# Sixteen stores of a transformer block issued by ScalarE instead of SyncE

## The chip, the cores and the metric

The kernel runs on one core of a Trainium2 chip. Its time is device microseconds of one launch. Before the change it takes 1237.1 us, the median of three runs (1236.84 to 1238.23). A run is told from no change here from about 0.2% on, 2.5 us.

A core has five engines with an instruction stream each, and each stream runs strictly in its own order. The profile calls them PE (TensorE, matrix products; its weight loads are listed as PEld), DVE (VectorE), ACT (ScalarE), POOL (GpSimd) and SP (SyncE, which in this kernel only issues transfers). "SPq" is SyncE's stream of transfer issues.

## The reference

One block over 1024 tokens of width 1024, all float32. It is cut here to what the change touches.

```python
h = rmsnorm(x, g_mix_pre[l])
proj = h @ w_in[l]
qa, ka, va, gate_a, beta_a, alpha_a, qb, kb, vb = jnp.split(proj, split_at, axis=-1)
out_a = gated_deltanet(qa, ka, va, gate_a, beta_a, alpha_a, ...)   # 4 heads of 128
out_b = dilated_attention(qb, kb, vb, rel_bias)                    # 8 heads of 64
mix = jnp.concatenate([out_a, out_b], axis=-1) @ w_out[l]
x = x + rmsnorm(mix, g_mix_post[l])
...
# inside gated_deltanet: a scan over 16 chunks of 64 tokens, then
_, o = lax.scan(step, s0, (u, w, attn, q_dec, k_dec, g_end))
o = o * lax.rsqrt(jnp.mean(o * o, axis=-1, keepdims=True) + RMS_EPS) * onorm_g
o = o * jax.nn.silu(heads(gate))
return o.reshape(Bn, S, GDN_WIDTH)
```

After the mix comes a gated feed-forward layer of width 2816. Two results matter below: the scan's normed output, and the SILU of the gate, with which it is multiplied.

## The kernel before, in words

Every matrix product takes its operands as a high and a low float32r part and sums three products of them, so most of the element-wise work consists of pairs "cast to the high part, subtract to get the low part". The tiles of 128 tokens are numbered t = 0 to 7.

**How the order comes about.** Each piece of work is a Python generator that yields one instruction after another. A planner (class Weaver) runs them all side by side when the program is built: it keeps a clock for each engine and a clock "D" for transfers, prices each instruction (class Op), and always emits the one that can start first by its clocks, ties going to the smaller priority number. Where a step may run on either of two engines (Either), it takes the one that would finish it first. The order in which the planner emits is the order in which each engine runs on the chip. A transfer's price on the issuing engine stands in one line, 166: 565 ns for SyncE and 1000 ns for anyone else. Before the change all 865 transfers are issued by SyncE, in one stream, so a transfer that waits for its data holds up all transfers emitted after it.

**The stages around the change**, with the times of the profiled execution:

- Projections (from the start to about 482 us): products of the normed input with w_in into PSUM tiles named pj. The last ones are the four gate heads in two halves, eight tiles gst of 128 x 512. They also serve as filler for TensorE beside the next stage.
- The scan (chain, lines 1388 to 1427, about 290 to 443 us): for each tile t the inputs ckq, cg, cbv and ckd are loaded; the recurrence alternates TensorE (p), VectorE (R, the state, o) and ScalarE (vn, parts of o). chain_out (lines 1434 to 1455) then squares and norms o, transposes it on TensorE (otp), has ScalarE copy it with the gain onorm into ot (two activations), and stores ot to d_mix in HBM. There is one ot buffer, shared with the squares osq.
- Attention (lines 1465 to 1667, about 290 to 525 us) beside it: loads qs, ks, strip, vn, vo and vf; scores pS, a VectorE reduction into Sr and mx, the exponential on ScalarE, transposes tp, casts ptn, pto and ptf, the value products pV, and sums plow and ptmp, stored to d_mix as well.
- Gates (lines 811 to 851): VectorE multiplies each projected tile into gst. When six are there, gate_silu runs six SILUs on ScalarE in one go and then stores six tiles to d_gt; when all eight are there, the other two follow. The first tile's gates are also used straight from SBUF.
- Output projection (lines 1694 to 1862, from about 485 us): w_out is loaded into borrowed buffers (y, gpost, gpre, wor), cast to woh and wol; d_mix and d_gt come back as mx and gt; the attention's part is divided by its sums (rtok, rt, rrow, rp); the products are pw.
- Then the residual and the norm, and the feed-forward layer (tiles bank) to the end.

The stores of ot wait for nobody until mix_load reads them back, one tile at a time, from 448.0 us on; those of gst are read back from 495.6 us on.

Of the kernel before, what the change touches and what calls it, by code (L numbers as in the profile page):

```python
# [21 lines left out]
P = 128  # L22
S = 1024
# [69 lines left out]
def _free(ap):  # L93
    n = 1
    for d in ap.shape[1:]:
        n *= d
    return n


def _run(ap):  # L100

    dims = [list(d) for d in ap.ap]
    n, dims = 1, dims if ap.space == DRAM else dims[1:]
    for st, k in reversed(dims):
        if k > 1 and st != n:
            break
        n *= k
    return n
# [34 lines left out]
class Op:  # L143


    def __init__(self, w, eng, name, fn, args, kw):
        self.eng, self.fn, self.args, self.kw = eng, fn, args, kw
        out = kw.get("out", args[0] if args else None)
        outs = [out] + ([kw["accum_out"]] if kw.get("accum_out") is not None else [])
        ins = [x for x in list(args) + list(kw.values())  # L150
               if isinstance(x, bass.AP) and not any(x is o for o in outs)]
        self.dma = name == "dma_start"
        self.table = next((x for x in args if x in (AF.Exp, AF.Silu)), None) if name == "activation" else None
        self.grow = name == "matmul" and not kw.get("start", True)
        self.ins, self.outs = [w.region(x) for x in ins], [w.region(x) for x in outs]
        n = max(_free(x) for x in ins + outs)
        if eng == "PE":
            if name == "transpose":
                c = 109.0
            elif args[2].dtype == F32R:  # L160
                c = max(_free(args[2]), 256) * 0.4414 + 3.0
            else:
                n = _free(args[2])
                c = n * 1.667 if out.shape[0] == P else 36 + 0.44 * n if n <= 64 else n * 1.0 if out.shape[0] == 64 else n * 0.45
        elif self.dma:
            c = 565.0 if eng == "S" else 1000.0
            b = 4 * min(_run(x) for x in ins + outs)
            self.move = 4.0 * _free(out) * out.shape[0] / b * (10.0 + b / 22.0) / 16.0
        elif eng == "A":
            c = 60 + (1.87 if any(x.ap[-1][0] > 3 for x in ins) else 0.83 if any(x.space == PSUM for x in ins) else 0.9) * n + 93 * (len(outs) - 1) + 85 * sum(1 for x in ins if _free(x) == 1)  # L170
        elif eng == "G":
            vals = list(args) + list(kw.values())
            c = 295 + 165.0 * n if ALU.pow in vals else (60 + 0.83 * n if name == "memset" else 140 + (1.7 if any(d[0] == 0 for x in ins for d in x.ap) else 2.1) * n)
        elif name in ("tensor_scalar", "tensor_copy", "memset") and not any(x.space == PSUM for x in ins):
            c = 65 + 0.52 * n + (60 if any(_free(x) == 1 for x in ins) and n > 1 else 0)
        elif any(abs(x.ap[-1][0]) > 3 for x in ins + outs):
            c = 65 + 1.85 * n
        elif name == "reciprocal":
            c = 70 + 8.0 * (n - 1)
        else:  # L180
            c = 65 + 1.04 * n + (60 if name == "scalar_tensor_tensor" else 0)
        self.cost, self.bias = c, 0.0

        self.rows = (args[1].shape[0], out.shape[0]) if eng == "PE" else None
        sb = sum(1 for x in ins if x.space != PSUM and _free(x) > 1)
        self.port = not self.dma and (eng == "G" and sb > 0 or eng == "V" and (
            sb > 1 or name in ("tensor_scalar", "tensor_copy") and all(x.space != PSUM for x in ins + outs) and _free(out) > 1))
# [350 lines left out]
def block_kernel(ctx: ExitStack, tc: tile.TileContext, a, out):  # L538
    nc = tc.nc
    w = Weaver(nc)  # L540
    T, V, A, G, SY = (Engine(w, e, k) for e, k in (
        (nc.tensor, "PE"), (nc.vector, "V"), (nc.scalar, "A"), (nc.gpsimd, "G"), (nc.sync, "S")))
# [5 lines left out]
    def tr(out, in_):  # L548
        return T.transpose(out, in_, ident[:])
# [33 lines left out]
    def rstd_from(pool, ss, scale, eps, tag, bufs=4):  # L583
        n = ss.shape[-1]
        m = pool.tile([P, n], F32, name=tag + "_m", bufs=bufs)
        yield V.tensor_scalar(m[:], ss, scale, eps, ALU.mult, ALU.add)
        r = pool.tile([P, n], F32, name=tag + "_r", bufs=bufs)
        yield G.tensor_tensor(r[:], m[:], mhalf[:, :n], ALU.pow)
        return r
# [6 lines left out]
    d_mix = dr.tile([KT, P, S], F32, name="d_mix")  # L596
# [214 lines left out]
    def gate(*hs):  # L811
        def sink(h, hf, ps):
            z = yield gstS[h // 2, hf].get([P, 512], F32, name="gst")
            yield V.tensor_tensor(z[:], ps[:], rb[:, hf * 512:hf * 512 + 512], ALU.mult)
            pj.put(ps)
            gates.append((z, d_gt[h, :, hf * 512:hf * 512 + 512]))
            if not hf:
                first[h] = z
            if len(gates) in BURST:
                w.spawn(gate_silu(gates[len(silued):]), 2, eager=len(gates) in EAGER)  # L820
                silued.extend(gates[len(silued):])
            if len(gates) == 8:
                ev_gates.fire()
        for hf in range(2):
            for h in hs:
                yield from proj_half(12 + h, hf, lambda hf, ps, h=h: sink(h, hf, ps))
            if len(hs) > 1:
                for b in range(2):
                    hS.put(*hT[b, hf])
# [10 lines left out]
    def gate_silu(part):  # L840
        yield [A.activation(z[:], z[:], AF.Silu) for z, _ in part]
        for z, dst in part:
            silu.add(z.tensor.name)
        if len(first) == GH and all(z.tensor.name in silu for z in first.values()):
            ev_silu.fire()
        for z, dst in part:
            yield SY.dma_start(dst, z[:])
            if z not in first.values():
                outS.put(z)
        if part[-1] is gates[-1] and len(gates) == 8:  # L850
            ev_gt.fire()
# [536 lines left out]
    def chain():  # L1388
        for t in range(NT):
# [4 lines left out]
            for c in range(2):  # L1394
# [30 lines left out]
                cp.put(p2)  # L1425
            ch.put(kq, gg, kd, bv)
            w.spawn(chain_out(o, t), 3)

    def chain_o1(o, p1, sw, us):
# [4 lines left out]
    def chain_out(o, t):  # L1434
        sq = yield ch.get([P, GH, P], F32, name="osq", tag="ot", bufs=1)
        yield A.activation(sq[:], o[:], AF.Square)
        ss = ch.tile([P, GH], F32, name="oss")
        yield V.tensor_reduce(ss[:], sq[:], AX.X, ALU.add)
        ch.put(sq)
        yield V.tensor_tensor(ss[:], ss[:], rqs2[:, t::8], ALU.mult)  # L1440
        r = yield from rstd_from(ch, ss[:], 1.0, EPS, "on", 2)
        yield V.tensor_tensor(r[:], r[:], rqsw[:, t::8], ALU.mult)
        yield V.tensor_tensor(o[:], o[:], r[:].unsqueeze(2).broadcast_to([P, GH, P]), ALU.mult)
        yield After(o[:])
        tp = yield banks.get([P, GH, 2, 64], F32, name="otp")
        yield [tr(tp[:, h, :, :], o[:, h, :]) for h in range(GH)]
        ch.put(o)
        ot = yield ch.get([P, GH, 2, 64], F32, name="ot", bufs=1)
        for c in range(2):
            yield A.activation(ot[:, :, c, :], tp[:, :, 1 - c, :], AF.Copy, scale=onorm[:])  # L1450
        banks.put(tp)
        yield SY.dma_start(d_mix[0:4, :, t * P:(t + 1) * P].rearrange("h p j -> p h j"),
                           ot[:].rearrange("p h c j -> p h (c j)"))
        ch.put(ot)
        ev_o[t].fire()
# [1016 lines left out]
```

## Time and profile before

| | |
|---|---|
| time, median of 3 runs | 1237.1 us (1236.84 to 1238.23) |
| time of the profiled execution | 1238.43 us |
| its span, first to last instruction | 1236.7 us |
| granted clock of TensorE, mean | 0.998 |
| transfers, moved in all | 865 issues by SyncE, 213.42 MB |
| ot stores to d_mix | 8 of 256 KB, from 306.3 to 442.8 us |
| gst stores to d_gt | 8 of 256 KB, from 469.5 to 491.5 us |

The profile gives busy time for each engine and for chosen stretches ("windows": PE, PEld, DVE, ACT and POOL busy us with the number of instructions, then TensorE's granted clock, the transfer engines' busy share and GB/s). A row of waits reads: who waited, for whose instruction, total us, times, longest. A row of a timeline reads: start, duration, engine, line, operation, output<-input, shape, count, and in brackets the idle time before it and what ended it. The chain of waits follows the work that ended last backwards from the end; its rows read start, duration, what. Nearly every row carries line 283, because the planner issues everything through that one line; so one goes by the names of the tiles. The duration of a transfer's issue is the time of the issuing engine only, not that of the movement.

### The profile page before, as it was taken

Reading aid. Unit: us, or ns where it says so; the run is one execution under the profiler, and the core shown is the slowest. Engines: PE = TensorE matmul, PEld = TensorE weight load, DVE = VectorE, ACT = ScalarE, POOL = GpSimd, SP = SyncE. Lnnn points to the kernel's source line nnn. Section 1 sums busy time; section 2 is a strip of 40 time slices with the busy share of each in tenths; the row PEclk is TensorE's granted clock in tenths of the full one; section 3 lists DMA queues with packets and bytes.
Section 4 is the critical chain, followed back from the end, with each engine's and each line's share of the span. In section 5 each row is a group of like instructions: output and inputs, shape, how many; then the busy total and the mean of one; then the engine's idle time right before and its main releaser. Section 6 shows DMA issues by size and latency. Waiting matters only on the chain.

```text
span 1236.7 us, 19617 instructions
## 1 busy us (share of the span) xinstructions
PE 1213.7 (98%) x6783; PEld 1015.4 (82%) x6783; DVE 962.2 (78%) x1857; ACT 575.5 (47%) x1174; POOL 190.6 (15%) x159
## 2 busy tenths in 40 slices
PE   7999999999999998999999999999999999999997
PEld 6887798888888887888788888888888887888886
DVE  4689969737999887876898877876678767976876
ACT  6545432236677757655553333333333334544541
POOL 0135321011221102111210010111001100000111
PEclk9999999999999999999999999999999999999999
DMA  7754372769877578694544433322333129744335
GB/s 261 240 154 158 111 220 83 176 213 306 251 234 255 160 235 255 201 297 158 188 142 154 137 120 128 107 72 85 120 128 120 50 94 327 247 134 153 101 121 204
DMA packets 169978, 213.42 MB, mean 173 GB/s; under 512 B 32232, under 2 KB 87016, under 8 KB 169880
## 3 DMA queue, kind: packets, MB, share of 16 engines
q1 hardware_dynamic: 169880, 212.18, 54.2%
q8 instruction: 54, 0.88, 0.3%
q14 instruction: 44, 0.36, 0.1%
HBM read 149.97 MB, written 65.95 MB: 175 GB/s over the span
## 4 chain that ended last, share of the span: by engine, by line
PE 87%; DVE 5%; DMA 4%; ACT 2%; issue 1%; POOL 1%; SPq 1%; DVEq 0%; POOLq 0%; ACTq 0%
PE bank L283 48%; PE pj L283 19%; PE pw L283 7%; PE tp L283 4%; PE p L283 3%; PE pS L283 2%; PE pV L283 2%; PE pm L283 2%; DMA xn<-in_x 1%; DMA gpre<-in_w_out 1%; SPq L283 1%; DMA ks<-d_k 0%; DMA views<-in_w_down 0%; DMA wr<-in_w_in 0%; DMA xT<-in_x_t 0%
## 5 line engine op out<-in xcount | busy, mean ns | idle before, releaser
L283 PE MATMUL pj<-hTh,w 128*128 128x512 f32 x768 | 265.9, 403 | 6.2 <-ACT hTh L283 5.3
L283 PEld LDWEIGHTS pj<-hTh,w 128*128 128x128 f32 x768 | 145.7, 190 | 37.7 <-ACT hTh L283 5.3
L283 ACT CAST wbh<-wraw 128x512 fp32r<-128x512 f32 x131 | 80.9, 622 | 199.2 <-PE bank L283 126.1
L283 PE MATMUL pj<-hTl,w 128*128 128x512 f32 x384 | 151.5, 395 | 0.0
L283 DVE TENSOR_TENSOR wbl<-wraw,wbh 128x512 fp32r<-128x512 f32 x131 | 94.1, 721 | 29.2 <-ACT wbh L283 29.1
L283 PE MATMUL bank<-views 128*128 128x512 f32 (+1 forms) x307 | 85.0, 385 | 0.0
L283 PEld LDWEIGHTS pj<-hTl,w 128*128 128x128 f32 x384 | 73.0, 190 | 11.8 <-DVE hTl L283 0.7
L283 PE MATMUL bank<-views,dah 128*128 128x512 f32 (+1 forms) x214 | 73.5, 379 | 0.0
L283 PE MATMUL bank<-dbh,views 128*128 128x512 f32 (+1 forms) x201 | 70.3, 380 | 0.0
L283 POOL TENSOR_TENSOR m<-m,m 128x512 f32<-128x512 f32 x18 | 28.3, 1574 | 251.9 <-DVE r L283 153.3
L283 PEld LDWEIGHTS bank<-views 128*128 128x128 f32 x307 | 57.4, 188 | 11.7 <-ACT views L283 0.4
L283 PE MATMUL pw<-woh,mh 128*128 128x512 f32 x128 | 51.5, 403 | 0.0
L283 PE MATMUL pw<-woh,ml 128*128 128x512 f32 x128 | 50.0, 391 | 0.0
L283 PE MATMUL pw<-wol,mh 128*128 128x512 f32 x128 | 49.9, 390 | 0.0
L283 PE MATMUL bank<-dbh,dah 128*128 128x512 f32 (+1 forms) x129 | 49.1, 381 | 0.0
L283 ACT CAST w<-wr 128x512 fp32r<-128x512 f32 x54 | 33.2, 619 | 33.9 <-PE pj L283 25.0
L283 DVE SCALAR_TENSOR_TENSOR yc<-raw,convw,yc 128x1024 f32<-128x1024 f32 x36 | 47.3, 1313 | 0.4
L283 PEld LDWEIGHTS bank<-views,dah 128*128 128x128 f32 x214 | 40.0, 188 | 7.6
L283 ACT ACTIVATE Sr<-Sr,mx 128x384 f32<-128x384 f32 (+2 forms) x64 | 38.2, 598 | 13.7 <-DVE mx L283 12.4
L283 DVE TENSOR_TENSOR w<-wr,w 128x512 fp32r<-128x512 f32 x39 | 26.5, 687 | 23.1 <-ACT w L283 22.9
L283 DVE TENSOR_TENSOR m<-bank,m 128x512 f32<-128x512 f32 x44 | 30.1, 685 | 18.2 <-PE bank L283 18.2
L283 PEld LDWEIGHTS bank<-dbh,views 128*128 128x128 f32 x201 | 37.6, 188 | 7.2
(405 smaller groups left out, 3278.1 us busy)
## 6 DMA issues: line engine op xcount, KB each, us to landing
wr<-in_w_in SPq DMA_DIRECT2D x56, 256.0 KB
wraw<-in_w_gate SPq DMA_DIRECT2D x52, 256.0 KB
wraw<-in_w_up SPq DMA_DIRECT2D x52, 256.0 KB
views<-d_hid SPq DMA_DIRECT2D x47, 256.0 KB
db<-in_w_down SPq DMA_DIRECT2D x40, 256.0 KB
qs<-d_q SPq DMA_DIRECT2D x64, 128.0 KB
da<-d_hid SPq DMA_DIRECT2D x30, 256.0 KB
d_hid<-x SPq DMA_DIRECT2D x22, 256.0 KB
```

The source lines that it names most:

```text
L283: op.fn(*op.args, **op.kw)
```

## The change

Two stores are issued by ScalarE (A) instead of SyncE (SY), and the planner is given a price of 450 ns for a transfer issued by ScalarE, where it would have been 1000. What is stored, where to and after which instruction stays the same. Since the planner works with the new engine and price, the order of everything that it emits after the first of these stores may come out differently on all engines.

```diff
@@ -163,7 +163,7 @@
         elif self.dma:
-            c = 565.0 if eng == "S" else 1000.0
+            c = {"S": 565.0, "A": 450.0}.get(eng, 1000.0)
             b = 4 * min(_run(x) for x in ins + outs)
@@ -844,7 +844,7 @@
         for z, dst in part:
-            yield SY.dma_start(dst, z[:])
+            yield A.dma_start(dst, z[:])
             if z not in first.values():
                 outS.put(z)
@@ -1449,7 +1449,7 @@
         banks.put(tp)
-        yield SY.dma_start(d_mix[0:4, :, t * P:(t + 1) * P].rearrange("h p j -> p h j"),
+        yield A.dma_start(d_mix[0:4, :, t * P:(t + 1) * P].rearrange("h p j -> p h j"),
                            ot[:].rearrange("p h c j -> p h (c j)"))
         ch.put(ot)
         ev_o[t].fire()
```

## The prediction

> **What bounds the kernel now.** I read the page first, then TensorE's waits, the busy table by stretches, the chain and the timelines around the sixteen stores. Busy shares come first.
>
> ```profile
> PE 1213.7 (98%) x6783; PEld 1015.4 (82%) x6783; DVE 962.2 (78%) x1857; ACT 575.5 (47%) x1174; POOL 190.6 (15%) x159
> PE 87%; DVE 5%; DMA 4%; ACT 2%; issue 1%; POOL 1%; SPq 1%; DVEq 0%; POOLq 0%; ACTq 0%
> ```
>
> TensorE is busy 1213.7 of 1236.7 us and carries 87% of the chain. Whatever moves between ScalarE and SyncE can gain at most TensorE's 23.0 us of idle time, so I look for where that idle time is.
>
> ```profile
> core 0: us, PE busy (x) PEld busy (x) DVE busy (x) ACT busy (x) POOL busy (x), PEclk, DMA share, GB/s
> 300.00:445.00 145.00, 144.40 (x1164) 125.10 (x1163) 133.22 (x415) 101.52 (x293) 27.37 (x25) 1.00 0.74 228
> 480.00:500.00 20.00, 16.16 (x104) 13.36 (x106) 18.42 (x45) 16.24 (x39) 5.36 (x4) 0.91 0.79 254
> 650.00:1230.00 580.00, 578.86 (x2583) 479.78 (x2581) 441.21 (x681) 217.76 (x390) 59.95 (x44) 1.00 0.42 137
> PE rt L283 <- POOL rtok L283: 3.8, 1, 3.8
> ```
>
> The scan with the attention beside it (300 to 445 us) leaves TensorE 0.60 us idle, and 650 to 1230 leaves 1.14. The only hole near the change is between 480 and 500: 3.84 us, in one wait, with a granted clock of 0.91 in that stretch. What fills the time before that hole is in the chain.
>
> ```profile
> 468.98 7.51 DMA gpre<-in_w_out
> ...
> 477.09 1.64 ACT kf L283 x2
> ...
> 486.39 0.33 PE rt L283
> ```
>
> A weight load into gpre, issued at 468.98, lands 7.51 us later; ScalarE casts it (woh) and then works off, kf copies and all, what TensorE's rt waits for. So one short stretch, about 455 to 486 us, is not bound by TensorE but by a load and by ScalarE's order. The gate stores lie in it.
>
> **The change part by part.** Sixteen issues move: eight of the scan's output (d_mix) and eight gates (d_gt).
>
> ```profile
> L283 SPq DMA_DIRECT2D d_mix<-ot x8: 365/374/378, 306.3 to 442.8; - x8
> L283 SPq DMA_DIRECT2D d_gt<-gst x8: 326/448/912, 469.5 to 491.5; - x8
> ```
>
> *Issue time.* By the medians this is 8 x 0.374 + 8 x 0.448 = 6.6 us that SyncE loses and ScalarE gains. No row shows a transfer issued by ScalarE, so SyncE's rows are the nearest; by the fastest and slowest of each row the sum lies between 5.5 and 10.3 us. Eight of them, 3.0 us, fall in 300 to 445, where ScalarE is idle for 145.00 - 101.52 = 43.5 us: 0 on the path. If that cover were gone the 3.0 us would be paid in full. Six gate stores, 6 x 0.448 = 2.7 us, come right after the six SILUs of the first burst:
>
> ```profile
> 468.23 3.24 ACT L283 ACTIVATE gst<-gst 128x512 f32<-128x512 f32 x6
> 476.56 0.62 ACT L283 CAST woh<-gpre 128x512 fp32r<-128x512 f32 x1 [5.09 <-DMA gpre<-in_w_out]
> 490.31 1.15 ACT L283 ACTIVATE gst<-gst 128x512 f32<-128x512 f32 x2
> ```
>
> ```profile
> 490.98 5.53 PE pw L283 x24
> ```
>
> ScalarE sits idle for 5.09 us there, waiting for gpre, so the 2.7 us are hidden in that wait: 0, and 2.7 if the planner gives that cast to VectorE. The last two stores, 0.9 us, hold up the casts behind 490.31, while TensorE, in the chain's row, has 24 projection matmuls up to 496.51 in hand: 0.
>
> *ScalarE's own result.* A store on ScalarE waits for the activation just before it to be written. The nearest row is SyncE's: the two ot of 430.29 end at 431.13 and the store starts at 431.16, so 0.03 us; from the other side, a queued instruction behind it may be held some 0.3 us as well. Sixteen times that is 0.5 to 5 us of ScalarE time under the same cover: 0.
>
> ```profile
> 430.29 0.84 ACT L283 ACTIVATE ot<-otp,onorm 128x256 f32<-128x256 f32 x2 [0.20 <-PE otp L283]
> 431.16 0.38 SPq L283 DMA_DIRECT2D d_mix<-ot  x1
> ```
>
> *The turn of eight.* The transfers keep a distance of eight: SyncE's store of the first scan tile stood until the eighth transfer before it had landed.
>
> ```profile
> 297.28 0.92 SPq L283 DMA_DIRECT2D cbv<-d_bv  x1
> 298.31 3.80 SPq L283 DMA_DIRECT2D qs<-d_q  x4
> 302.26 1.17 SPq L283 DMA_DIRECT2D ks<-d_k  x2
> 304.33 0.33 SPq L283 DMA_DIRECT2D strip<-d_bias  x1
> 306.26 0.38 SPq L283 DMA_DIRECT2D d_mix<-ot  x1
> SPq L283 <- DMA cbv<-d_bv: 1.5, 1, 1.5
> ```
>
> From cbv to strip there are 1 + 4 + 2 + 1 = 8, and the wait before 306.26 is for cbv. I take it that a transfer issued by ScalarE takes its turn among the same eight; then ScalarE is held, and everything queued on it behind the store: the casts ptn and pto, the exponentials Sr, the scan's vn.
>
> ```profile
> 300.61 0.84 ACT L283 ACTIVATE ot<-otp,onorm 128x256 f32<-128x256 f32 x2 [0.51 <-PE otp L283]
> 309.63 0.58 ACT L283 COPY vn<-p 64x512 f32<-64x512 f32 x1
> 310.68 1.05 PE L283 MATMUL p<-vn,ckd 128*128 128x128 f32 x8
> 301.40:309.63 8.23, 8.23 (x81) 6.76 (x79) 8.04 (x25) 5.16 (x17) 1.05 (x1) 1.00 0.97 287
> ```
>
> The worst case for this tile: ot ends at 301.45, the hold lasts until 306.2 and the issue 0.4, so 5.2 us. ScalarE has 8.23 - 5.16 = 3.1 us idle before vn, which leaves vn 2.1 us late; TensorE needs it 0.47 us after its end (310.21 to 310.68), so it loses up to 1.6 us. The best case is 0: the store is issued behind a few more instructions, or earlier in the transfers' turn. For the other fifteen the transfer eight back had landed before the result was there, so SyncE's wait, where it had one, was for ScalarE. I take 0.5 of 0 to 1.6 us, near the lower end because TensorE has filler from the projections in this stage.
>
> *What SyncE gains.* Its waits for these results end, and the loads queued behind the stores start earlier.
>
> ```profile
> SPq L283 <- ACT ot L283: 7.3, 3, 5.5
> SPq L283 <- ACT gst L283: 1.9, 3, 0.9
> ```
>
> 9.2 us of standing go from SyncE, 5.5 of them in one piece ahead of the load at 431.63. But TensorE's idle time in that stage is 0.60 us, so the gain is between 0 and 0.6: 0.
>
> *The load of gpre.* Now gpre is ahead of the six gate stores in one queue:
>
> ```profile
> q1 hardware_dynamic: 169880, 212.18, 54.2%
> 468.39 0.54 SPq L283 DMA_DIRECT2D strip<-d_bias  x1
> 468.98 0.42 SPq L283 DMA_DIRECT2D gpre<-in_w_out  x1
> 469.49 4.36 SPq L283 DMA_DIRECT2D d_gt<-gst  x6
> strip<-d_bias SPq DMA_DIRECT2D x10, 416.0 KB
> gpre<-in_w_out SPq DMA_DIRECT2D x1, 512.0 KB
> d_gt<-gst SPq DMA_DIRECT2D x8, 256.0 KB
> 471.50:476.50 5.00, 5.00 (x42) 3.94 (x42) 3.68 (x16) 0.00 (x0) 3.17 (x3) 1.00 0.94 297
> ```
>
> From 471.5 to 476.5 the engines moved 5.0 x 297 = 1.49 MB at a share of 0.94, so there is no room left. What is ahead, strip with 0.43 MB and gpre with 0.52, is at most 0.95, so at least 0.5 MB of the stores had already run beside it on engines that were done with gpre. Six stores are 6 x 256 KB = 1.57 MB. After the change they stand in a queue of ScalarE's own. If they stay behind gpre, as now, gpre lands as now: 0. If all the rest of them goes ahead of it, it lands (1.57 - 0.54) / 0.297 = 3.5 us later, and TensorE's hole grows by as much. Against this, ScalarE can do the two kf copies (1.64 us, now behind the wait) ahead of the cast. So -1.6 to +3.5; I take +0.5, as stores issued from 471.5 on come 2.5 us after gpre was queued. The Trainium skill, page "DMA: Bandwidth & Descriptors", section "Queues, rings and completion order", says that each DMA engine goes round-robin, packet by packet, between the queues that have work for it, and that SyncE and ScalarE have a queue each. By that rule gpre shares from 471.5 on, the term would be near its upper end, and the sum would come out near 1241; no row of before can show it, as there is one queue.
>
> *The order.* The planner's price for a transfer of ScalarE's, 450 ns, costs nothing by itself, but from the first store on a new order is worked out for all engines. Later stretches have only 1.14 us to win; I count 0, with 2 us either way.
>
> The sum: 0.5 + 0.5 = +1.0 us. The profiled execution took 1238.43 us, 1.73 beyond its span and 1.33 above the median of 1237.1; its sum would be 1239.4. Against the median this gives 1238.1 us. About 0.2%, or 2.5 us, is what a measurement can tell from no change, so this is no difference.
>
> **The rivals.** *The stores delay gpre (slower).* Place: the hole before rt. Price: up to 3.5 us on gpre, one for one on TensorE, since ScalarE's work behind woh has no other slack up to 486.39; with the 0.5 of the first tile +3 to +4, so 1240.1 to 1241.1 us. It decides from the point where gpre lands over 2.5 us later than 7.51 after its issue. For it: the share of 0.94, and the rule of taking turns above. Against: gpre's head start. Chance 0.24.
>
> *ScalarE is held by the turn of eight in several tiles (slower).* For it: each hold stops an engine on which the recurrence waits, and a transfer can take as long as gpre to land, 7.51 us. Against: only one of the sixteen waited on it at SyncE. Two or three tiles at 1.6 us make 1240.3 to 1241.9. Chance 0.09.
>
> *The hole closes (faster).* With the cast of gpre off the head of ScalarE's queue, or the stores fully inside the idle 5.09 us and the later casts on VectorE, rt starts 3.1 to 3.84 us earlier, and the slower clock after the hole (0.91 over 20 us is 1.8 us at most) can go with it: 1237.1 - 3.1 = 1234 down to 1237.1 - 5.6 = 1231.5. For it: the hole is the largest wait of TensorE's near the change, and the planner sees ScalarE's clock 2.7 us later just there. Against: VectorE would then stand before gpre, and it is busy 18.42 of 20 us behind it. Chance 0.25.
>
> *The change does nothing that shows:* my forecast, 0.42, its own range 1235 to 1239.6.
>
> **How the numbers follow.** Faster by over 0.2% is the closing hole, 0.25; slower are the two delays, 0.24 + 0.09 = 0.33; the rest, 0.42, is no difference. The range goes from the middle of the closed hole, 1232.5, to just above the delays, 1242.5; it leaves out the lower half of the first and some double mishaps, under 2 in 10.
>
> **What would show it.** Right: sixteen issues on ScalarE of 0.35 to 0.5 us, a second transfer queue of 4.2 MB, no SyncE wait for ot or gst, TensorE idle in 300 to 445 under 3 us, rt's wait of 2 to 5 us. Wrong: gpre landing after 10 us or more, ScalarE waiting for landed transfers ahead of its stores, rt without a wait, or a TensorE loss after 500 us that only the new order explains.

## The result, and the profile after

After the change the kernel takes 1243.6 us (median of 6 runs, 1241.05 to 1245.16); before, beside it, 1237.2 (6 runs, 1236.57 to 1238.52). The ratio is 1.0046, with a 95% interval of 1.0036 to 1.0056: slower, by 5.7 us as a ratio and 6.4 as medians. The forecast was 1238.1, and the range ended at 1242.5. The profiled execution took 1243.91 us with a span of 1241.9, 5.2 us longer than that of before. It repeated on other chips at 1.0023 and 1.0049 (below), so its size is some 0.2 to 0.5%.

From the page of after, the busy shares, then the queues (packets, MB, share of the transfer engines' time):

```profile
PE 1216.6 (98%) x6783; PEld 1017.5 (82%) x6783; DVE 967.1 (78%) x1874; ACT 573.4 (46%) x1161; POOL 179.0 (14%) x155
...
q1 hardware_dynamic: 164504, 207.98, 52.9%
q10 hardware_dynamic: 5376, 4.20, 1.0%
```

TensorE's busy time grew by 2.9 us (1216.6 against 1213.7) for the same 6783 products, and its idle time from 23.0 to 25.3. There is a second queue with the 4.2 MB of the sixteen stores. What they cost ScalarE is in the groups of the two tiles (ns: fastest, median, slowest):

```profile
L283 ACTq DMA_DIRECT2D d_mix<-ot x8: 366/380/407, 300.5 to 443.3; - x8
```

```profile
L283 ACTq DMA_DIRECT2D d_gt<-gst x8: 326/352/742, 471.4 to 493.6; - x8
```

The stretches of after answer to those of before:

```profile
300.00:445.00 145.00, 143.56 (x1156) 124.41 (x1154) 134.79 (x413) 98.18 (x277) 28.70 (x26) 1.00 0.72 218
480.00:500.00 20.00, 15.71 (x70) 13.00 (x69) 15.46 (x30) 16.37 (x34) 4.50 (x4) 0.83 0.84 264
600.00:650.00 50.00, 47.96 (x207) 38.69 (x206) 48.02 (x80) 31.00 (x58) 7.00 (x5) 0.97 0.47 161
650.00:1230.00 580.00, 580.00 (x2577) 480.89 (x2576) 440.80 (x676) 219.47 (x391) 58.21 (x42) 1.00 0.42 137
```

In 300 to 445 TensorE now stands for 1.44 us (before 0.60), in 480 to 500 for 4.29 (before 3.84). In that stretch the granted clock is 0.83 instead of 0.91, and 0.97 in 600 to 650, where before had 1.00. Worked out from these, the lower clock costs 20 x 0.08 + 50 x 0.03 = 3.1 us, about the growth in busy time (2.9). So in this profile the loss is made of holes, and of the slow stretch that follows a hole. Which holes, TensorE's waits from 290 to 650 us tell:

```profile
PE rp L283 <- ACT rrow L283: 4.3, 1, 4.3
PE tp L283 <- DVE y L283: 3.2, 3, 2.0
PE pS L283 <- DVE ptn L283: 1.6, 1, 1.6
PE tp L283 <- DVE ptf L283: 0.9, 2, 0.8
```

The wait of 3.8 us for rtok, the hole of before, is gone. A hole of 4.3 us stands a few instructions further on, at rp, which waits for ScalarE's cast rrow. What made rrow late is read backwards in the timelines of after:

```profile
467.45 4.06 SPq L283 DMA_DIRECT2D qs<-d_q  x4
473.20 2.28 SPq L283 DMA_DIRECT2D ks<-d_k  x2
475.70 0.59 SPq L283 DMA_DIRECT2D strip<-d_bias  x1
476.34 0.55 SPq L283 DMA_DIRECT2D gpre<-in_w_out  x1
...
471.38 0.34 ACTq L283 DMA_DIRECT2D d_gt<-gst  x1
...
473.49 1.77 ACTq L283 DMA_DIRECT2D d_gt<-gst  x3
482.04 1.63 ACT L283 COPY kf<-ks 128x512 f32<-128x512 f32 x2 [8.08 <-DMA ks<-d_k]
...
486.46 1.58 ACT L283 CAST rrow<-rt 32x128 fp32r<-32x128 f32 x4
...
480.23 0.28 PE L283 MATMUL rt<-ident,rtok 128*128 128x128 f32 x1
486.87 1.12 PE L283 MATMUL rp<-rrow,spread 128*128 128x128 f32 x4 [4.29 <-ACT rrow L283]
```

rt starts 6.2 us earlier than before (480.23 against 486.39). But ScalarE stands for 8.08 us at the copy kf, until the second load of ks has landed, and rrow is queued behind it. In before these two ks went out together right behind qs, and kf did not wait for them. Here the row of the two issues lasts 2.28 us: the first goes out at 473.20, the second only at 475.04, 0.02 us after the first gate store, which ScalarE had issued at 471.38, had landed. SyncE's waits name such stores, in 400 to 500 us and in the scan's first tile:

```profile
SPq L283 <- DMA d_gt<-gst: 2.5, 4, 1.4
```

```profile
SPq L283 <- DMA d_mix<-ot: 4.9, 1, 4.9
```

The completion semaphore that the trace gives for each transfer says how. All 865 transfers, whichever of these two engines issues them, take eight completion semaphores in turn, and an issue waits until the transfer eight turns ahead of it has landed. ScalarE's first scan store has turn 217, and SyncE's load with turn 225 is one of the qs of that tile. The first, second and third of the gate stores have turns 415, 417 and 419; ks, strip and a store of ptmp have 423, 425 and 427. So it is SyncE above all that is held, by ScalarE's stores. ScalarE's third gate store also stood 0.6 us, for SyncE's load of gpost, but the activations ran on meanwhile. The turns that the stores take bring SyncE's own transfers round sooner, too: ahead of that second ks, the last qs and the first ks stood 1.8 and 1.7 us for a vn and a ptmp of SyncE's own. In the first tile SyncE's timeline shows the hold:

```profile
297.17 9.50 SPq L283 DMA_DIRECT2D qs<-d_q  x4
306.71 1.23 SPq L283 DMA_DIRECT2D ks<-d_k  x2
```

Before, the four qs took 3.80 us and ks followed at 302.26; now they take 9.50 and ks comes at 306.71.

### The profile page after: what moved, and what is told of

It reads as the page before. It is cut to its first block, busy times and chain, and to the rows that moved or that the text cites. A ratio compares the mean times of both kernels' runs of the same rounds, so it can differ in the third digit from the quotient of the medians.

```text
span 1241.9 us, 19591 instructions
## 1 busy us (share of the span) xinstructions
PE 1216.6 (98%) x6783; PEld 1017.5 (82%) x6783; DVE 967.1 (78%) x1874; ACT 573.4 (46%) x1161; POOL 179.0 (14%) x155
## 4 chain that ended last, share of the span: by engine, by line
PE 49%; DVE 1%; issue 0%; POOL 0%; ACT 0%; DVEq 0%; POOLq 0%; ACTq 0%
PE bank L283 49%; DVE x L283 0%; DVE acc L283 0%; POOL n_r L283 0%; ACT jk L283 0%; DVEq L2468 0%; PE tp L283 0%; DVE y L283 0%; DVE fg L283 0%; DVE n_m L283 0%; POOLq L2468 0%; POOLq L283 0%; ACTq L283 0%
## 5 line engine op out<-in xcount | busy, mean ns | idle before, releaser
L283 PE MATMUL bank<-views 128*128 128x512 f32 (+1 forms) x291 | 82.0, 384 | 0.0
L283 PE MATMUL bank<-views,dah 128*128 128x512 f32 (+1 forms) x226 | 77.5, 380 | 0.0
L283 PE MATMUL bank<-dbh,views 128*128 128x512 f32 (+1 forms) x217 | 75.8, 380 | 0.0
L283 PEld LDWEIGHTS bank<-views 128*128 128x128 f32 x291 | 54.5, 188 | 10.8
L283 PEld LDWEIGHTS bank<-dbh,views 128*128 128x128 f32 x217 | 40.6, 188 | 7.7
```

The costliest lines, as they stand in the source:

```text
L283: op.fn(*op.args, **op.kw)
```

## The experiments

Two things changed at once: who issues, and the planner's order from the first store on. The kernels separate them, in three orders: the old one, the new one, and a third that another price gives. TensorE's idle time from 280 to 660 us (380 less its busy time in that stretch of each profile) stands beside each ratio to before, and so does SyncE's longest wait for the first scan store to land. Each ratio is to before, timed beside it on the same chip; the rows come from several chips, and one kernel's ratio moved by up to 0.0026 between them (after: 1.0023 to 1.0049). Executions of one kernel lie within some 3 us of their median, a few farther off, and already ahead of the first moved store one profile runs up to 2.6 us ahead of another. So places are read from the profiles and sizes from the ratios.

| order, issuer of the sixteen stores | TensorE idle, us | first store's hold, us | ratio to before, 95% |
|---|---|---|---|
| old, SyncE (before, twice) | 6.4, 5.7 | none | control 1.0004 (0.9991 to 1.0017) |
| old, ScalarE | 8.4 | 5.7 | 1.0023 (1.0009 to 1.0037) |
| old, ScalarE but for the first | 6.9 | none | 1.0019 (1.0007 to 1.0031) |
| old, GpSimd | 9.0 | none | 1.0018 (1.0007 to 1.0030) |
| new, SyncE (twice) | 8.8, 8.0 | none | 1.0025 (1.0014 to 1.0035), 1.0018 (1.0009 to 1.0028) |
| new, scan ScalarE, gates SyncE | 9.9 | 5.1 | 1.0010 (0.9995 to 1.0024) |
| new, scan SyncE, gates ScalarE | 9.0 | none | 1.0032 (1.0020 to 1.0044) |
| new, GpSimd | 7.6 | none | 1.0027 (1.0014 to 1.0040) |
| new, ScalarE (after, three times) | 10.5, 9.1, 10.6 | 4.9, 5.0, 4.9 | 1.0046 (1.0036 to 1.0056), 1.0023 (1.0010 to 1.0037), 1.0049 (1.0034 to 1.0064) |
| third, SyncE | 2.5 | none | 0.9967 (0.9956 to 0.9979) |
| third, ScalarE | 4.8 | 4.7 | 0.9996 (0.9986 to 1.0006) |
| third, GpSimd | 3.9 | none | 0.9985 (0.9977 to 0.9994) |
| own order, only the scan's stores | 7.5 | 5.1 | 0.9999 (0.9987 to 1.0011) |
| own order, only the gates' | 4.2 | none | 0.9988 (0.9973 to 1.0002) |

### Engine without order, order without engine

The old order on every engine, stores by ScalarE:

```diff
+    AS = Engine(w, nc.scalar, "S")
-            yield SY.dma_start(dst, z[:])
+            yield AS.dma_start(dst, z[:])
-        yield SY.dma_start(d_mix[0:4, ...
+        yield AS.dma_start(d_mix[0:4, ...
```

> The order of the kernel before, kept on every engine, with only the sixteen stores taken out of SyncE's stream and put into ScalarE's at the same place of the order. Turn theory (all transfers take turns among eight completion semaphores; the new order puts loads of the attention between the gate stores, so that they wait for ScalarE's stores to land): here the loads ks, strip and gpre stand ahead of the gate stores as before, so no loss: 1235 to 1239 us. Rival, a second queue whose stores take the transfer engines from gpre: gpre lands 2 us or more later than 7.5 us after its issue and the time is 1239 to 1242. Rival, ScalarE's own issue time: 16 x 0.4 us partly in the way, 1239 to 1243.

Its first tile, SyncE's timeline, and TensorE's wait there:

```profile
298.10 8.59 SPq L283 DMA_DIRECT2D qs<-d_q  x4
306.73 1.23 SPq L283 DMA_DIRECT2D ks<-d_k  x2
```

```profile
PE tp L283 <- DVE ptf L283: 1.9, 1, 1.9
```

It is slower by 0.23%. The four qs are stretched as in after, and TensorE has a hole of 1.9 us in the first tile that before does not have. The turn of eight had been expected to cost nothing here; it does, at the first scan store, and the clock follows the hole (before is busy for all 10.00 us of this stretch, at 1.00):

```profile
310.00:320.00 10.00, 8.45 (x41) 7.38 (x42) 9.53 (x29) 6.50 (x16) 2.02 (x2) 0.83 0.87 292
```

The time, 1239.3 us, fits the ranges of both rivals. But gpre lands 6.48 us after its issue, no later than before's 7.51, so the rival of gpre is out.

The new order on every engine, stores by SyncE, planned as if by ScalarE:

```diff
+    SA = Engine(w, nc.sync, "A")
-            yield A.dma_start(dst, z[:])
+            yield SA.dma_start(dst, z[:])
-        yield A.dma_start(d_mix[0:4, ...
+        yield SA.dma_start(d_mix[0:4, ...
```

> The order of the kernel after, kept on every engine, with the sixteen stores issued by SyncE again. Turn theory and the theory that the new order costs by itself: the loads still stand between the gate stores, now even in one line with them, so the loss stays: 1241 to 1246 us. Rivals second queue and ScalarE's issue time: both are gone, so 1236 to 1239.

ScalarE's timeline and TensorE's waits (440 to 520 us) of this kernel:

```profile
477.91 1.70 ACT L283 COPY kf<-ks 128x512 f32<-128x512 f32 x2 [2.52 <-DMA ks<-d_k]
```

```profile
PE pV L283 <- DVE gst L283: 1.5, 1, 1.5
PE pS L283 <- DVE ptn L283: 1.5, 1, 1.5
```

Without ScalarE's stores kf waits 2.52 us instead of 8.08, and rp does not wait at all. Yet the ratio is 1.0025: the order loses by itself, in several holes of up to 2 us. The time, 1239.3 us, lies between the two ranges that had been expected.

### One half of the stores, planned anew

Each of the two edits alone, with the new price:

```diff
# scan_only: the gate stores go back
-            yield A.dma_start(dst, z[:])
+            yield SY.dma_start(dst, z[:])
# gates_only: the scan stores go back
-        yield A.dma_start(d_mix[0:4, ...
+        yield SY.dma_start(d_mix[0:4, ...
```

> Only the eight stores of the scan's output on ScalarE. Turn theory: the one 4.9 us wait of SyncE for the first store stays, TensorE loses 1 to 2 us up to 320 us, the gates' stage is as before: 1237 to 1240 us. If any new order costs: anything from 1237 to 1244.

> Only the eight gate stores on ScalarE; the order is the old one up to about 470 us. Turn theory: the loads of the attention are planned between the stores again and wait for them, ScalarE's kf waits 5 to 8 us for ks, 1239 to 1243 us. Rival ScalarE's issue time: 8 x 0.35 us at most, 1237 to 1239.

Neither differs from before clear of noise, both lie under the ranges of the turn theory, and each has an order of its own, so they say nothing of the two halves of after. They do say that a store issued by ScalarE need not make the kernel slower. With the gates alone ScalarE itself is held: its fifth gate store goes out at 473.97, when its own first, eight turns ahead, has landed, and kf stands behind it:

```profile
474.87 1.68 ACT L283 COPY kf<-ks 128x512 f32<-128x512 f32 x2 [3.07 <-DMA d_gt<-gst]
```

### The first scan store

The old order with fifteen stores by ScalarE, and with all sixteen by GpSimd:

```diff
-        yield AS.dma_start(d_mix[0:4, ...
+        yield (AS if t else SY).dma_start(d_mix[0:4, ...
```

```diff
+    GS = Engine(w, nc.gpsimd, "S")
-            yield AS.dma_start(dst, z[:])
+            yield GS.dma_start(dst, z[:])
-        yield AS.dma_start(d_mix[0:4, ...
+        yield GS.dma_start(d_mix[0:4, ...
```

> The order of before on every engine; fifteen of the sixteen stores issued by ScalarE, the first scan store by SyncE. Theory of the turn (the first scan store takes a turn ahead of SyncE's loads, and the load eight turns later has to wait until it has landed): the 3.7 us that the old order with all sixteen on ScalarE lost in the first tile are gone, so a ratio of 0.9985 to 1.0010 against before, and qs of the first tile issued no more than 0.5 us later than in before. Rival (ScalarE pays for each issue, or a second queue costs): fifteen sixteenths of the loss stay, 1.0015 to 1.003.

> The order of before; all sixteen stores issued by GpSimd, whose transfers do not take the eight turns that SyncE and ScalarE share. Theory of the turn: SyncE's loads wait for none of these stores, no loss in the first tile, 0.9985 to 1.0010. Rival (a second queue beside the loads takes their bandwidth, whoever issues): the loss of the old order on ScalarE stays, 1.0015 to 1.0035. By either, GpSimd pays for its issues, at a price that no run has shown yet; it stood idle for 85% of before.

The hold is gone from both profiles, with the hole in the first tile. The times are not: 1.0019 and 1.0018. So the hold is real and its hole too, but without it the ratio is no better; on this the theory of the turn failed twice. The profiles show where a lead can go. All kernels of the old order run TensorE's products in one order. Its 3157th product starts at 450.01 us in before and at 448.56 in the kernel with fifteen stores, but rt starts at 486.39 and 486.28 (486.28 with GpSimd, 486.46 in the second profile of before). So in these profiles what is gained ahead of the gates' stage is lost again there. In the stretch 445 to 460 us, just behind the last scan store, the GpSimd kernel has two waits of TensorE's where before has none:

```profile
PE pS L283 <- DMA vo<-d_v: 0.7, 1, 0.7
PE pS L283 <- DVE mx L283: 0.5, 1, 0.5
```

GpSimd's kernel in the third order (below) has both again, with 0.7 us each, and SyncE's there has neither. The last scan store is no direct cause of them: it had landed at 444.91 and 444.51, ahead of the loads that TensorE waits for there. Their cause is open.

### The two halves in the new order

```diff
# new_order_gates_sync
-            yield A.dma_start(dst, z[:])
+            yield SA.dma_start(dst, z[:])
# new_order_scan_sync
-        yield A.dma_start(d_mix[0:4, ...
+        yield SA.dma_start(d_mix[0:4, ...
```

> The order of after; the scan's eight stores issued by ScalarE, the eight gate stores by SyncE, planned as if by ScalarE. Theory of the turn: the gates' stage has no ks that waits for a landed gate store, so the 4 to 5 us that after lost between the first output products and the first third of the up-projection go down to the 0 to 3 of the new order on SyncE: 1238 to 1240, a ratio of 1.001 to 1.003, with ks landed by 477 and no hole of 4 us at rp or rt. Rival (the new order costs, whoever issues): as after, 1.0035 to 1.006.

> The order of after; the gate stores issued by ScalarE, the scan's stores by SyncE, planned as if by ScalarE. The gate stores have the turns that they have in after (415, 417, 419 ahead of ks at 423). Theory of the turn: ks is again issued when store 415 has landed, ScalarE waits for ks some 8 us, and TensorE has its hole of 4 us at rp, while the first tile loses under 0.5 us: 1240 to 1243, a ratio of 1.003 to 1.005. Rival (the damage is done in the first tile and carried on): about as the new order on SyncE alone, 1.0015 to 1.003, without the wait for ks.

With the gates on SyncE there is no hole at rp, and the first tile keeps its hold, with a hole of 1.0 us. With the gates on ScalarE the first tile is clean, and ScalarE's timeline and TensorE's wait at rp are these:

```profile
477.60 1.67 ACT L283 COPY kf<-ks 128x512 f32<-128x512 f32 x2 [4.61 <-DMA d_gt<-gst]
```

```profile
PE rp L283 <- ACT rrow L283: 0.9, 1, 0.9
```

The wait for ks is there, but 4.6 us and not 8, and the hole is 0.9 us and not 4. (The bracket names the gate store because ks, turn 423, tells of its landing by the same semaphore; ks landed at 477.52.) The direction held and the size did not. ks (turn 423) was again issued 0.02 us after the landing of store 415, but in this execution it took 4.3 us to land instead of 6.9.

### The same stores by GpSimd, and after again

```diff
+    GA = Engine(w, nc.gpsimd, "A")
-            yield A.dma_start(dst, z[:])
+            yield GA.dma_start(dst, z[:])
-        yield A.dma_start(d_mix[0:4, ...
+        yield GA.dma_start(d_mix[0:4, ...
```

> The order of after; all sixteen stores issued by GpSimd, planned as if by ScalarE, so that none of them takes one of the eight turns of the loads. Theory of the turn: SyncE's ks in the gates' stage waits for no gate store, ScalarE waits for ks under 4 us, and the time falls to that of the new order alone, 1.001 to 1.003. Rival (the stores, in a queue beside the loads, take their bandwidth): as after, 1.0035 to 1.006, with ks issued before 474 but landing after 480.

> The kernel after, unchanged, beside the others on one chip. Every theory: 1.0035 to 1.006. If the hold of ks by landed gate stores is the program's and not one execution's, the profile shows again store 415 landing, ks (turn 423) issued within 0.1 us of that, a wait of ScalarE for ks of 6 to 9 us, and a hole of TensorE of 3 to 5 us at rp or rt; if not, the hole is elsewhere or under 2 us while the time stays.

> The kernel before, unchanged, as a control. Every theory: a ratio of 0.999 to 1.001. Its profile tells how much the places of the losses depend on the one profile of before that the others were read against: in that one TensorE reached its thousandth projection product at 288.2 us, in the others at 286.1 to 288.5. If this one is there near 286.5 and ends 1 to 2 us before 1236.7, the losses of the others counted from their own start hold; if it ends near 1236.7 all the same, an early start is lost again by the gates' stage whatever the kernel.

The copy kf in the GpSimd kernel, and in after's second and third profile (third below), each with its wait:

```profile
475.63 1.70 ACT L283 COPY kf<-ks 128x512 f32<-128x512 f32 x2 [2.14 <-DMA ks<-d_k]
```

```profile
480.13 1.65 ACT L283 COPY kf<-ks 128x512 f32<-128x512 f32 x2 [6.85 <-DMA ks<-d_k]
```

```profile
479.41 1.65 ACT L283 COPY kf<-ks 128x512 f32<-128x512 f32 x2 [6.50 <-DMA ks<-d_k]
```

The gate stores move the same bytes in all of these, also in a queue of their own with GpSimd. What differs is that GpSimd's stores do not take the loads' turns. There kf waits 2.14 us and rp not at all, and both ks go out ahead of the first gate store (472.41), not between and behind them:

```profile
469.70 1.19 SPq L283 DMA_DIRECT2D ks<-d_k  x2
```

So the late issue of ks is the work of the turn: that is shown. Beside the stores, ks then also takes longer to land (6.92 us in after, 5.23 here). In after's profiles the late ks is there each time, with holes at rp of 4.3, 3.1 and 2.7 us. But the medians of GpSimd's kernel and of after were equal on this chip (1240.14 and 1240.16), and after, at 1.0023, came out under its expected range; so it left open how much of after's time the hold is. The control came out at 1.0004; its profile was as late at the start as the first (288.7 us), so this run could not tell whether an early start is lost again.

### Does any new order cost?

Stores on SyncE, with every store to d_mix and d_gt priced 450 ns instead of 565:

```diff
-            c = 565.0 if eng == "S" else 1000.0
+            c = (450.0 if "d_mix" in str(out.tensor.name) or "d_gt" in str(out.tensor.name) else 565.0) if eng == "S" else 1000.0
```

> Every store to d_mix and d_gt stays on SyncE and is priced 450 ns in the planner instead of 565: another order, and no transfer of ScalarE's. If the order of before is a chance best and nearly any new order costs, as the order of after does with all stores on SyncE (1.0025): 1.001 to 1.004. If orders differ by no more than a measurement can tell: 0.999 to 1.001.

It gains 0.33%: 1233.2 us against 1237.1, which neither range had. TensorE does not stand in the stretch of the old hole:

```profile
480.00:500.00 20.00, 20.00 (x135) 16.46 (x134) 16.45 (x44) 14.66 (x33) 2.65 (x2) 1.00 0.86 263
```

So with all stores on SyncE orders differ by 0.2 to 0.3% to either side, and that of before is no chance best. This version beats both kernels.

### Order and engine side by side

After and the new order on SyncE, unchanged, on one chip, and the third order with the stores moved:

```diff
# price_450_scalar; price_450_gpsimd has GS in place of AS
-            yield SY.dma_start(dst, z[:])
+            yield AS.dma_start(dst, z[:])
-        yield SY.dma_start(d_mix[0:4, ...
+        yield AS.dma_start(d_mix[0:4, ...
```

> The kernel after, unchanged, on the chip on which the next one runs too: it stood at 1.0046 on one chip and at 1.0023 on another. If the issuing engine costs beside the order: 1.0035 to 1.006, above the next kernel by 0.001 to 0.003. If nearly all of it is the order: 1.002 to 1.0035, within 0.001 of the next. By either, the profile shows ks (turn 423) issued when store 415 has landed, and TensorE's hole at rp of 1 to 4.5 us.

> The order of after with every store issued by SyncE, once more, beside after on one chip. Order alone: 1.0015 to 1.0035. If the first measurement of 1.0025 was high by chance: under 1.0015, and then the issuing engine carries most of what after loses.

> The order of the kernel that priced its stores 450 ns on SyncE (0.9967), unchanged; the sixteen stores issued by ScalarE. The stores' turns are 217 and 419 to 427, ahead of none of the ks loads of the gates' stage. If moving the stores off SyncE costs by itself, as in the order of before (1.0018 to 1.0023 with ScalarE, fifteen of sixteen on ScalarE, or GpSimd): 0.998 to 1.0. If it costs only where a load is held or a hole is near: 0.996 to 0.9975.

> The same order, the sixteen stores issued by GpSimd, which leaves the eight turns to SyncE's loads. If moving the stores off SyncE costs by itself, whoever issues them: 0.998 to 1.0, as with ScalarE. If ScalarE's turn is what costs: 0.996 to 0.9975, and the ScalarE kernel above it.

After is at 1.0049 and the same order on SyncE at 1.0018, with intervals that do not meet: the engine costs 0.3% there and the order 0.2%. In the third order the kernel with ScalarE stands 0.3% above that with SyncE (0.9996 and 0.9967) and the one with GpSimd 0.2% (0.9985). But SyncE's was timed on another chip, and the intervals of GpSimd's and SyncE's meet, so that 0.2% is not shown. ScalarE's profile shows the hold at the first scan store again, and SyncE's and GpSimd's do not:

```profile
SPq L283 <- DMA d_mix<-ot: 4.7, 1, 4.7
```

## Why the prediction was wrong

*Issue time:* right. Sixteen issues of 0.380 and 0.352 us by the medians are 5.9 us (predicted 6.6), and no wait of TensorE's from 290 to 650 us is put down to them.

*ScalarE's own result:* right. In after the first store starts 0.03 us after the activation that makes its data:

```profile
299.67 0.84 ACT L283 ACTIVATE ot<-otp,onorm 128x256 f32<-128x256 f32 x2 [0.53 <-PE otp L283]
300.54 0.39 ACTq L283 DMA_DIRECT2D d_mix<-ot  x1
```

No run shows the 0.3 us that was taken as the other bound; the term is 0 without it.

*The turn of eight:* this step failed. "I take it that a transfer issued by ScalarE takes its turn among the same eight" was right. "Then ScalarE is held, and everything queued on it behind the store" was the wrong way round in after: the first store went out at once, and SyncE's loads eight turns later were held until it had landed. (ScalarE's hold was 0.6 us at one gate store of after, and over 1 us only in two other orders, for ScalarE's own stores: kf waits 3.07 us with the gates alone, and 1.02 us in the third order.) I looked at which transfer lies eight ahead of each store, and never at which lies eight behind. The store of ScalarE's stands far ahead of SyncE's backlog in the turn, so the loads behind it wait for something that has only just been made. In the first tile the upper end of 1.6 us was about the size (holes of 0.7 to 1.9 us where ScalarE issued that store), but by another mechanism, so that is luck. At the gates, where I had put nothing, it delayed ks and made the hole at rp of 2.7 to 4.3 us.

*What SyncE gains:* right in that nothing came of it. Its waits for ot and gst as results are gone, and waits for their landing took their place (4.9 and 2.5 us; before has none and 1.5).

*The load of gpre, and its rival:* the cast of gpre was not late. In the trace of after the load lands 7.66 us after its issue, against 7.51, so the term of +0.5 was nothing, and the rival failed in the load that it named. Of its kind it came true: a load on the path delayed by the gate stores, 2.7 to 4.3 us, near its price of 3.5. It was ks, not gpre. The rule of the Trainium skill that I cited, page "DMA: Bandwidth & Descriptors", section "Queues, rings and completion order", that the transfer engines take the queues in turn, fits the second ks, 4.07 us from issue to landing in before and 6.92 in after, with five gate stores under way. It is not isolated here, since the same load took 5.36 and 4.64 us in the new order on SyncE, with no other queue; and the hold ahead of its issue is beside that rule.

*The hole closes:* rt does start early, as this rival had it, and in the new order on SyncE the longest wait left around it is 1.5 us (1.7 in its second profile). ScalarE's stores gave it back at rp, one wait further on. Of the signs listed as speaking against the forecast, "rt without a wait" is the one that came; TensorE's idle time in 300 to 445 did stay under 3 us.

*The order:* "0, with 2 us either way" was mis-sized. The new order costs 2.2 to 3.1 us (0.0018 and 0.0025 of 1237), in holes from 420 us on, and a third order gains 4 us. That spread of some 7 us is larger than the 5.7 us to be explained. As a size it is the second step that failed: 0 was taken for it, and it measured 2.2 to 3.1.

So after's loss is order and engine together: on the chip with both, 0.0018 and 0.0031 of 1236 us, 2.2 and 3.8. Of the engine's part, the hold of ks and the hole behind it are shown, with their mechanism. What stays open is why the stores cost 0.2% in the old order without the hold of the first tile, with GpSimd too, where the profiles show no new wait of over 1.5 us; and how after came to 1.0023 on one chip beside GpSimd's 1.0027.

## What to carry to other kernels

When a transfer moves to another engine, find out what it shares with the loads that stay: here a turn of eight, where a store that is issued at once can hold a load eight turns behind it until the store has landed. Look at who stands behind the moved instruction in every shared list, not only at what stands ahead of it. And where a planner reworks the order, measure the order by itself (the new order on the old engine) before giving the engine the credit or the blame: here orders alone were worth -0.33% to +0.25%.

## What the runs showed of the hardware

A store issued by ScalarE overlaps the activation that is running. In the timeline of after, ScalarE's issue and its next activations:

```profile
328.74 0.36 ACT L283 ACTIVATE o<-p,egsw 64x128 f32<-64x128 f32 x1 [0.39 <-DVE R L283]
328.80 0.40 ACTq L283 DMA_DIRECT2D d_mix<-ot  x1
329.00 0.86 ACT L283 ACTIVATE o<-p,egsw 64x128 f32<-64x128 f32 x3
```

The issue lasts from 328.80 to 329.20, with activations running from 328.74 on, the next one from 329.00. So moving an issue to ScalarE takes next to nothing from its arithmetic.

A hole can be paid twice, the second time through the clock. These stretches of after stand around the hole at 487 us (TensorE's granted clock is the third number from the right):

```profile
485.00:490.00 5.00, 3.13 (x9) 2.67 (x10) 4.92 (x10) 4.93 (x14) 0.54 (x1) 0.62 0.82 234
490.00:495.00 5.00, 5.00 (x21) 4.28 (x20) 4.57 (x10) 4.51 (x9) 0.95 (x2) 0.70 0.88 302
```

5 x 0.38 + 5 x 0.30 = 3.4 us of clock are missing there, which is all that 0.83 over 20 us takes away. And a hole of one length can cost this or nothing. Around the wait of about 2 us for y, before and then after:

```profile
605.00:615.00 10.00, 8.06 (x40) 6.40 (x40) 9.52 (x17) 5.71 (x14) 3.62 (x3) 1.00 0.57 187
615.00:625.00 10.00, 10.00 (x46) 8.28 (x45) 9.96 (x16) 7.85 (x14) 3.55 (x2) 1.00 0.26 81
```

```profile
605.00:615.00 10.00, 8.12 (x35) 6.11 (x33) 9.12 (x16) 5.20 (x12) 3.69 (x3) 1.00 0.63 218
615.00:625.00 10.00, 9.85 (x41) 8.12 (x42) 9.93 (x18) 6.80 (x13) 1.63 (x1) 0.83 0.29 100
```

TensorE is idle for some 1.9 us in both first stretches; behind it the clock stays at 1.00 in one and drops to 0.83 over 10 us, 1.7 us' worth, in the other. No run was made on what decides that.
